# Two paddings in SBUF: 96 bytes at its right end and 64 in the pool of constants

## The chip, the cores and the metric

One core of a Trainium2 chip runs the whole kernel as one launch. The metric is the time of one execution in microseconds of the device. TensorE (PE) multiplies, its weight loads (PEld) run beside the matmuls, VectorE (DVE), ScalarE (ACT) and GpSimd (POOL) do the elementwise work, and nearly all DMAs are issued by the SP queue.

## The reference, cut to what matters

One layer over 2048 latent tokens and 256 context tokens, width 1024, 8 heads of 128:

```python
hx = layernorm(x) * (1 + scale_x) + shift_x          # ctx likewise, with c_ctx
px = hx @ w_in + b_in                                # 10272 columns: q k v, z_a, decay logits, x_in, b_gate, c_gate, z_b, g_a, g_b
q, k, v = silu(conv3(qkv))                           # q and k normalised
o = gated_delta_rule(q, k, v, g, beta)               # both directions, from the context's final state
y_a = rmsnorm(o) * o_norm_w * silu(z_a)
y_b = b_gate * (conv3(c_gate * x_in) + conv_b_b) * silu(z_b)
merged = sigmoid(g_a) * (y_a @ w_a) + sigmoid(g_b) * (y_b @ w_b)
out = layernorm(2 ** 0.25 * x + gate_x * (merged @ w_out)) * ln_g + ln_b
```

## The kernel before

**Three stages.** After a start of about 100 us (shift and scale, normalised tokens, the first right-hand operands) `projections` multiplies by `w_in` until about 1840 us. Then `window` runs the delta-rule scan of 36 visits, with the products by `w_b` and `w_a` put between the scan's matmuls as fillers, until a little after 3000 us. Then `final` multiplies by `w_out` and normalises.

**A dense product** is made in float32r, with each operand split into a high and a low part, and costs three matmuls instead of one: high by high, high by low, low by high. One matmul has a stationary operand of 128 by 128, which a weight load brings into the array, and a moving operand of 128 by 512, which streams through it. Every matmul of a dense product has its own weight load.

**The projections** are made in Winograd's form by `strassen`: 80 units (40 for each pair of token tiles), each a pair of column tiles of `w_in`. A unit has seven products in the order `ORDER = "1675243"`, a product has four tiles of k, and each tile has the three matmuls of L743 to L745:

```python
mm(ps, hi[:, k, :], bh, ...)   # L743: stationary ah, moving bh
mm(ps, hi[:, k, :], bl, ...)   # L744: stationary ah, moving bl
mm(ps, lo[:, k, :], bh, ...)   # L745: stationary al, moving bh
```

That is 12 matmuls a product, 84 a unit and 6720 in all. The moving operands `bh`, `bl` of a product stay in SBUF through a pair's 40 units. Those of the products 1, 6, 7, 5 and 2 lie in pool `bp`, at the right end of SBUF; those of the products 4 and 3 (`LATE`) lie in pool `bq`, at the left. The stationary operands `ah`, `al` of the next unit are made while the current one runs, by ACT (the high part) and POOL (the low part) in `split`, in pool `ap`. The first 12 units of each pair give k, v and q; there PE also transposes what was finished (L1013), and for the values it makes the context's products in plain float32 (L792). The 28 units behind them give branch B and the gates.

**The fillers** (L1227, L1229, L1231; 1536 matmuls) have moving operands in pool `fa` and stationary ones in pool `wp`, both at the right end. The last products (L1574 to L1576; 672 matmuls) have moving operands in pool `bo` and stationary ones in `o0` and `o1`, all at the left. The scan's own matmuls are plain float32; each shows as two matmuls in the trace.

**What sets the addresses.** Pools are stacks: those of the left side grow up from the constants' pool `cp`, those of the right side grow down from the end of SBUF. A tile's *start* here is its byte offset within a partition, and its *phase* is that start modulo 128. As the tiles of the dense products have sizes that are multiples of 512 bytes, all tiles of one pool have the same phase.

Of the kernel before, what the change touches and what calls it, by code (L numbers as in the profile page):

```python
# [15 lines left out]
P = 128  # L16
D = 1024
KT = 8
H = 8
# [13 lines left out]
def bc(ap, n):  # L33
    """[p, a, 1] -> [p, a, n] by a zero stride."""
    return ap.to_broadcast([ap.shape[0], ap.shape[1], n])


class Kern:
# [6 lines left out]
    # ---------------------------------------------------------------- constants  # L45
    def consts(self, pool, tmp):
# [23 lines left out]
        # strict parts of a 16 x 16 block  # L70
# [5 lines left out]
        # inclusive causal masks [j, i]: 0 where kept, NEG elsewhere  # L76
# [9 lines left out]
    # ---------------------------------------------------------------- gated delta net  # L86
# [10 lines left out]
    def visit_load(self, v):  # L97
        """Loads of a chunk's keys, values, queries and running decays."""
# [21 lines left out]
    def visit_decay(self, v):  # L120
        """Decays: of every key to the chunk's end, of the state over the chunk, and between positions."""
# [23 lines left out]
    def gram(self, v, name, rhs):  # L145
        """Products of a chunk's keys, the same for both directions: kept in DRAM for the second."""
# [7 lines left out]
        for g in range(2):  # L154
# [4 lines left out]
            if v["latent"]:  # L159
                # with the other direction's strengths  # L160
# [9 lines left out]
    # R = (I + N)^-1 of each head's triangular N (its strict part; upper for d = 0)  # L170
    def inv_base(self, v):
        nc, g2, d, N = self.nc, self.g2, v["d"], v["N"]
        # the 32 x 32 diagonal blocks, negated
# [9 lines left out]
        # substitution within the 16 x 16 blocks  # L183
# [50 lines left out]
    def blocks(self, d, b):  # L234
        """(rows of the solved block, rows of the other) of every pair of b x b blocks."""
        lo, hi = (0, 1) if d == 0 else (1, 0)
        return [(slice(2 * b * g + b * lo, 2 * b * g + b * lo + b), slice(2 * b * g + b * hi, 2 * b * g + b * hi + b))
                for g in range(P // (2 * b))]
# [51 lines left out]
    # the recurrence  # L290
# [44 lines left out]
    # ---------------------------------------------------------------- dense helpers  # L335
    def load_w(self, src, c0, n=P):
        """W[:, c0:c0+n] as [128 k, 8, n], and its split into two float32r parts."""
# [11 lines left out]
    def split(self, hi, lo, src, eng=None):  # L349
        """hi + lo == src, each with the significant bits that a float32r pass carries."""  # L350
# [3 lines left out]
    def dense(self, ps, w, a, msl=slice(None), nsl=slice(None)):  # L354
        """ps[m, n] = sum_k w[k, m] a[k, n], operands in two float32r parts."""
# [7 lines left out]
    # ---------------------------------------------------------------- whole kernel  # L363
    def build(self, I, out):
# [3 lines left out]
        self.w_in = I["w_in"][0]  # L368
        cp = es.enter_context(tc.tile_pool(name="cp", bufs=1))
        dr = es.enter_context(tc.tile_pool(name="dr", bufs=1, space=DRAM))  # L370
# [37 lines left out]
        def settle():  # L408
            """Room for the scan."""
# [16 lines left out]
    # ---------------------------------------------------------------- the input projections  # L426
    def projections(self, es, eb, cp):
        """All products with w_in: the context's plainly, the latents' by pairs of token tiles (Winograd's form)."""
# [58 lines left out]
    def tokens_of(self, t):  # L487
        """A tile of latent tokens, two blocks at a time; the first where the second's operands will be."""
# [4 lines left out]
    def units(self, pair):  # L493
        """Column pairs of w_in in their order, each with what becomes of its four blocks
        and what comes before it and after it."""
        nc = self.nc
        cols = lambda seg, m: 4128 + seg * 1024 + m * P     # x_in, b_gate, c_gate, z_b, g_a, g_b
# [21 lines left out]
        # q, k, v; the context's values beside the latents'  # L519
# [14 lines left out]
        # branch B  # L534
# [50 lines left out]
        # gates  # L585
# [7 lines left out]
        for seg, dst in ((5, self.gb_d), (4, self.ga_d), (None, self.za_d)):  # L593
            for m in range(0, 8, 2):
                def evac(i, j, src, seg=seg, dst=dst, m=m):
                    b = (24 + m if seg is None else bcol(seg, m)) + i
                    zs = ph["ev"].tile([P, 512], F32, name="c11") if (i, j) == (0, 0) else src
                    if seg is None:
                        nc.scalar.activation(out=zs, in_=src, func=AF.Silu, bias=bT[:, b:b + 1])
                        # the last ones behind the activations, out of the way of the scan's loads  # L600
# [8 lines left out]
        if pair == 0:  # L609
            # the other pair's tokens, on the way  # L610
# [19 lines left out]
    # Winograd's form for C = W^T H with W^T = [[A11, A12], [A21, A22]] by (column tile, half of k) and  # L630
    # H = [[B11, B12], [B21, B22]] by (half of k, token tile):
    #   s1 = A21 + A22, s2 = s1 - A11, s3 = A11 - A21, s4 = A12 - s2
    #   t1 = B12 - B11, t2 = B22 - t1, t3 = B22 - B12, t4 = t2 - B21
    #   p1 = A11 B11, p2 = A12 B21, p3 = s4 B22, p4 = A22 t4, p5 = s1 t1, p6 = s2 t2, p7 = s3 t3
    #   C11 = p1 + p2, C12 = p1 + p6 + p5 + p3, C21 = p1 + p6 + p7 - p4, C22 = p1 + p6 + p7 + p5
    def prep_b(self, k):
        """The first pair's right-hand operands, a tile of k of each half."""
# [16 lines left out]
    def turn_pair(self, xs, q, k):  # L654
        """The second pair's operands of a block of tokens of each tile and a tile of k of each half, kept in DRAM."""
# [11 lines left out]
    def renew(self):  # L667
        """The second pair's operands in the place of the first's, each as soon as its last product is done."""
# [17 lines left out]
    def gate_rows(self, pool):  # L686
        """c's rows times the residual gate's columns of w_mod, by the two float32r parts of c."""
# [135 lines left out]
    def later(self, n, fn):  # L823
        """fn, n products from now."""
        self.due.append((self.tick + n, fn))
# [8 lines left out]
    # ---------------------------------------------------------------- startup  # L834
    def modulation(self, cp, wmp):
        """Small operands, the shifts and scales, and the first tokens."""
# [30 lines left out]
        # shift and scale: rows first, then channels on partitions; some tiles of k in float32r parts  # L867
# [756 lines left out]
```

## Time and profile before

| | us |
|---|---|
| median of 3 runs | 3305.19 |
| fastest and slowest | 3304.52, 3312.04 |
| span of the profiled execution | 3301.7 |
| PE busy in it | 3035.6 (92%) |
| DVE busy | 2283.1 (69%) |
| POOL busy | 1628.0 (49%) |
| ACT busy | 1561.9 (47%) |

The span is the time from the first to the last instruction. The time of the profiled execution as a whole is not listed apart; the shortest of the runs, 3304.52 us, is 2.8 us above the span, the median 3.5 us. Busy time of PE is a modelled one: matmuls overlap in the array, and one of 128x512 is shown as lasting about 0.39 us although the next one starts about 0.23 us after it. So the rate of a row of matmuls is read from their starts, in the timeline, and not from their durations.

### The profile page before, as it was taken

Reading aid. Unit: us, or ns where it says so; the run is one execution under the profiler, and the core shown is the slowest. Engines: PE = TensorE matmul, PEld = TensorE weight load, DVE = VectorE, ACT = ScalarE, POOL = GpSimd, SP = SyncE. Lnnn points to the kernel's source line nnn. Section 1 sums busy time; section 2 is a strip of 40 time slices with the busy share of each in tenths; the row PEclk is TensorE's granted clock in tenths of the full one; section 3 lists DMA queues with packets and bytes.
Section 4 is the critical chain, followed back from the end, with each engine's and each line's share of the span. In section 5 each row is a group of like instructions: output and inputs, shape, how many; then the busy total and the mean of one; then the engine's idle time right before and its main releaser. Section 6 shows DMA issues by size and latency. Waiting matters only on the chain.

```text
span 3301.7 us, 60541 instructions
## 1 busy us (share of the span) xinstructions
PE 3035.6 (92%) x22089; PEld 2484.4 (75%) x22089; DVE 2283.1 (69%) x5815; ACT 1561.9 (47%) x3453; POOL 1628.0 (49%) x1156
## 2 busy tenths in 40 slices
PE   7899999999998999999999888888889888898988
PEld 3677777788886777888878677887777777776766
DVE  7656545555646564555622678899898989978699
ACT  4664633333456555333434355555555665664321
POOL 3444557665576554666666333343343233424464
PEclk9999999999999999999999988889999989999999
DMA  5533322225564432222332654465566667667742
GB/s 210 142 99 96 95 80 87 74 64 156 173 186 136 115 93 76 64 64 65 98 108 86 214 172 150 167 196 170 174 205 212 212 216 239 219 209 241 228 146 102
DMA packets 423047, 481.75 MB, mean 146 GB/s; under 512 B 25428, under 2 KB 324949, under 8 KB 421724
## 3 DMA queue, kind: packets, MB, share of 16 engines
q1 hardware_dynamic: 413646, 470.43, 45.5%
q10 hardware_dynamic: 9102, 7.45, 0.7%
q8 instruction: 173, 2.83, 0.4%
q14 instruction: 126, 1.03, 0.1%
HBM read 341.32 MB, written 136.47 MB: 145 GB/s over the span
## 4 chain that ended last, share of the span: by engine, by line
PE 52%; DVE 25%; issue 6%; ACT 5%; DMA 5%; POOL 3%; SPq 1%; DVEq 0%; ACTq 0%; POOLq 0%
PE pd L743 13%; PE pd L744 13%; PE pd L745 13%; DVE gcb L140 3%; DVE rb L192 3%; DVE R L193 2%; POOL al L352 2%; DVE rb L191 2%; DMA gcb<-gcd 1%; PE pst L319 1%; ACT n L177 1%; POOL s L729 1%; DVE N L167 1%; PE pst L320 1%; DVE t L988 1%
## 5 line engine op out<-in xcount | busy, mean ns | idle before, releaser
L743 PE MATMUL pd<-bh,ah 128*128 128x512 f32 x2240 | 898.0, 401 | 9.8 <-ACT u L763 5.3
L745 PE MATMUL pd<-bh,al 128*128 128x512 f32 x2240 | 886.3, 396 | 0.0
L744 PE MATMUL pd<-bl,ah 128*128 128x512 f32 x2240 | 886.3, 396 | 0.0
L352 POOL TENSOR_TENSOR al<-s,ah 128x512 fp32r<-128x512 f32 x348 | 478.1, 1376 | 427.6 <-ACT ah L351 408.5
L352 POOL TENSOR_TENSOR al<-raw,ah 128x512 fp32r<-128x512 f32 x260 | 372.7, 1436 | 339.4 <-ACT ah L351 296.1
L743 PEld LDWEIGHTS pd<-bh,ah 128*128 128x128 f32 x2240 | 423.5, 189 | 107.2 <-issue 6.4
L745 PEld LDWEIGHTS pd<-bh,al 128*128 128x128 f32 x2240 | 423.5, 189 | 99.7 <-DVE al L352 0.4
L744 PEld LDWEIGHTS pd<-bl,ah 128*128 128x128 f32 x2240 | 424.0, 189 | 94.2
L351 ACT CAST ah<-s 128x512 fp32r<-128x512 f32 x352 | 215.0, 618 | 358.7 <-PE pd L744 342.8
L351 ACT CAST ah<-raw 128x512 fp32r<-128x512 f32 x264 | 162.5, 617 | 263.7 <-PE pd L744 213.8
L729 DVE TENSOR_TENSOR s<-s,raw 128x512 f32<-128x512 f32 x80 | 97.0, 1213 | 218.0 <-POOL s L729 161.5
L1231 PE MATMUL pf<-ah,wl 128*128 128x512 f32 x512 | 221.8, 433 | 6.7 <-DVE wl L352 4.6
L1227 PE MATMUL pf<-ah,wh 128*128 128x512 f32 x512 | 214.2, 419 | 12.4 <-DVE R L193 5.0
L1229 PE MATMUL pf<-al,wh 128*128 128x512 f32 x512 | 214.8, 420 | 5.9 <-POOL al L352 3.0
L352 POOL TENSOR_TENSOR wl<-wraw,wh 128x1024 fp32r<-128x1024 f32 x48 | 115.9, 2416 | 197.5 <-ACT wh L351 66.5
L192 DVE TENSOR_TENSOR rb<-rb,n 128x8 f32<-128x8 f32 (+6 forms) x540 | 200.8, 373 | 5.0
L140 DVE SCALAR_TENSOR_TENSOR gcb<-gcb,gc,mask 128x128 f32<-128x128 f32 x288 | 178.0, 623 | 9.1 <-ACT qd L137 8.1
L138 POOL TENSOR_TENSOR qd<-qd,qT 128x1024 f32<-128x1024 f32 x32 | 76.4, 2386 | 202.8 <-ACT qd L137 199.2
L193 DVE TENSOR_TENSOR R<-R,rb 128x8 f32<-128x8 f32 (+6 forms) x540 | 158.1, 294 | 5.6
L319 PE MATMUL pst<-S,qd 128*128 128x128 f32 x512 | 112.2, 304 | 33.7 <-ACT ot L1265 17.0
L768 DVE TENSOR_TENSOR u<-pd,u 128x512 f32<-128x512 f32 x80 | 55.0, 687 | 116.7 <-PE pd L745 113.6
L1005 ACT ACTIVATE t<-t 128x512 f32<-128x512 f32 (+1 forms) x112 | 67.3, 601 | 141.2 <-DVE t L990 141.2
(346 smaller groups left out, 6242.2 us busy)
## 6 DMA issues: line engine op xcount, KB each, us to landing
raw<-in_w_in SPq DMA_DIRECT2D x160, 512.0 KB, 4.0
kT<-kTd SPq DMA_DIRECT2D x36, 512.0 KB, 5.1
gcb<-gcd SPq DMA_DIRECT2D x36, 512.0 KB, 4.1
kt<-kd SPq DMA_DIRECT2D x36, 512.0 KB, 4.5
vh<-vd SPq DMA_DIRECT2D x36, 512.0 KB, 4.3
wraw<-in_w_b SPq DMA_DIRECT2D x32, 512.0 KB, 5.0
qT<-qTd SPq DMA_DIRECT2D x32, 512.0 KB, 3.9
wraw<-in_w_a SPq DMA_DIRECT2D x32, 512.0 KB, 5.2
```

The source lines that it names most:

```text
L140: nc.vector.scalar_tensor_tensor(out=gcb[:, h, :], in0=gcb[:, h, :], scalar=gcT[:, h:h + 1], in1=self.mask[d], op0=ALU.subtract, op1=ALU.min)
L192: nc.vector.tensor_tensor(out=rbv, in0=rbv, in1=bc(n16[:, :, i:i + 1], w), op=ALU.mult)
L193: nc.vector.tensor_tensor(out=R[:, :, c0:c1], in0=R[:, :, c0:c1], in1=rbv, op=ALU.add)
L319: nc.tensor.matmul(po[:, j, :], v["qd"][:, h, :], S[:, h, :], start=True, stop=False)
L351: self.nc.scalar.copy(out=hi, in_=src)
L352: (eng or self.nc.gpsimd).tensor_tensor(out=lo, in0=src, in1=hi.bitcast(F32), op=ALU.subtract)
L743: mm(ps, hi[:, k, :], bh, start=(first and k == 0), stop=False, skip_group_check=not first)
L744: mm(ps, hi[:, k, :], bl, start=False, stop=False, skip_group_check=not first)
L745: mm(ps, lo[:, k, :], bh, start=False, stop=(last and k == 3), skip_group_check=not first)
L1227: mm(ps, wh[:, k, :], ah, start=(k == 0), stop=False)
L1229: mm(ps, wh[:, k, :], al, start=False, stop=False)
L1231: mm(ps, wl[:, k, :], ah, start=False, stop=(k == KT - 1))
```

## The change

Two tiles are allocated that nothing writes or reads. One of 24 floats (96 bytes) is in a pool of its own at the right end of SBUF, opened ahead of all other pools. The other, of 16 floats (64 bytes), is the first in the pool of constants. Nothing else is changed but comments and docstrings, which are left out here:

```diff
     def build(self, I, out):
         tc, nc, es = self.tc, self.nc, self.es
         self.I = I
         x2 = I["x"][0]
         self.w_in = I["w_in"][0]
+
+        es.enter_context(tc.tile_pool(name="edge", bufs=1, side="right")).tile([P, 24], F32, name="edge")
         cp = es.enter_context(tc.tile_pool(name="cp", bufs=1))
+        cp.tile([P, 16], F32, name="cpad")
         dr = es.enter_context(tc.tile_pool(name="dr", bufs=1, space=DRAM))
```

On every engine the instructions, their order and their semaphores are the same in both programs, instruction by instruction. What differs is addresses: every tile of the left side starts 64 bytes higher, every tile of the right side 96 bytes lower. The phases, as the two built programs place the tiles:

| matmuls | moving, before → after | stationary, before → after |
|---|---|---|
| L743 to L745, products 1 6 7 5 2 (4800) | `bp` 96 → 0 | `ap` 64 → 0 |
| L743 to L745, products 4 3 (1920) | `bq` 64 → 0 | `ap` 64 → 0 |
| fillers (1536) | `fa` 96 → 0 | `wp` 96 → 0 |
| last products (672) | `bo` 64 → 0 | `o0`, `o1` 64 → 0 |
| L886, L887 at the start (24) | `wm` 0 → 32 | `cr4` in `cp` 16, 48, 112 → 80, 112, 48 |
| L792, the context's values, float32 | `hc` 96 → 0 | `ap` 64 → 0 |
| L1043, the context's keys, float32 | `hc` 96 → 0 | `wp` 96 → 0 |
| scan, float32: L299 / L319 | `S` 32 → 96 | `kT` 96 → 0 / `qd` 64 → 0 |

The constants in `cp` (the identity, the masks, the biases) move by 64, the scan's pool `g1` from 32 to 96, `g2` and `gb` from 64 to 0.

## Rows read from the trace of the kernel before

**Rows 1.** The page: its head, and groups of section 5 (columns as named there)

```profile
span 3301.7 us, 60541 instructions
...
L743 PE MATMUL pd<-bh,ah 128*128 128x512 f32 x2240 | 898.0, 401 | 9.8 <-ACT u L763 5.3
...
L744 PE MATMUL pd<-bl,ah 128*128 128x512 f32 x2240 | 886.3, 396 | 0.0
```

**Rows 2.** Busy time by stretch: us, PE, PEld, DVE, ACT, POOL, clock, DMA, GB/s

```profile
425.00:985.00 560.00, 559.53 (x2453) 450.22 (x2453) 302.92 (x438) 217.84 (x379) 367.60 (x269) 1.00 0.39 116
985.00:1312.00 327.00, 302.64 (x1364) 236.88 (x1363) 188.82 (x311) 186.10 (x497) 178.24 (x131) 0.97 0.38 107
1312.00:1841.00 529.00, 527.93 (x2275) 427.17 (x2275) 240.29 (x297) 188.21 (x303) 320.02 (x240) 1.00 0.28 84
```

**Rows 3.** Chain that ended last, by line, from 420 to 1850 us

```profile
by line: PE pd L743 27.7%; PE pd L744 27.7%; PE pd L745 27.6%; issue 3.7%; POOL al L352 2.0%; DVE t L988 1.4%; PE pd L1077 1.2%; POOL s L729 1.2%; DVE t L990 1.1%; PE pt L1013 1.0%; DVE t L1003 0.6%; DVE s L729 0.5%; PE pt L659 0.5%; ACT t 
```

**Rows 4.** Timeline of PE in one unit: start us, us, instruction

```profile
1448.19 0.40 PE L743 MATMUL pd<-bh,ah 128*128 128x512 f32 x1
...
1462.24 0.39 PE L743 MATMUL pd<-bh,ah 128*128 128x512 f32 x1
...
1463.62 0.39 PE L743 MATMUL pd<-bh,ah 128*128 128x512 f32 x1
...
1467.70 0.40 PE L743 MATMUL pd<-bh,ah 128*128 128x512 f32 x1
```

**Rows 5.** Busy time by stretch, columns as in rows 2: two products, then fillers

```profile
1459.43:1462.24 2.81, 2.81 (x13) 2.26 (x12) 0.75 (x1) 0.62 (x1) 2.59 (x3) 1.00 0.00 0
...
1465.00:1467.70 2.70, 2.70 (x13) 2.24 (x12) 0.75 (x1) 0.64 (x2) 1.29 (x1) 1.00 0.01 3
1860.77:1869.38 8.61, 8.61 (x39) 7.13 (x38) 8.37 (x28) 2.23 (x3) 4.78 (x2) 1.00 0.82 284
```

**Rows 6.** Timeline of PE: fillers in a row, from their second

```profile
1858.92 0.40 PE L1229 MATMUL pf<-al,wh 128*128 128x512 f32 x1
...
1860.77 0.39 PE L1227 MATMUL pf<-ah,wh 128*128 128x512 f32 x1
...
1869.38 0.39 PE L1231 MATMUL pf<-ah,wl 128*128 128x512 f32 x1
```

**Rows 7.** Timeline of PE: last products

```profile
3115.30 0.39 PE L1574 MATMUL po<-oh,ah 128*128 128x512 f32 x1
...
3117.57 0.39 PE L1575 MATMUL po<-ol,ah 128*128 128x512 f32 x1
```

**Rows 8.** Timeline of PE: plain float32, rows of equal matmuls merged

```profile
74.32 5.78 PE L1043 MATMUL pd<-hc,wraw 128*128 128x256 f32 x26
...
207.48 3.62 PE L792 MATMUL pd<-hc,raw 128*128 128x256 f32 x16
```

**Rows 9.** Waits of PE, 985 to 1312 us: waiter, waited for, us, times, longest

```profile
PE pt L1013 <- ACT t L1005: 17.0, 11, 3.9
```

**Rows 10.** Chain that ended last, by line, from 140 to 330 us

```profile
by line: issue 20.1%; PE pd L792 10.9%; POOL al L352 9.6%; PE pd L745 8.8%; PE pd L743 8.8%; PE pd L744 8.8%; POOL s L729 6.0%; DVE t L988 4.5%; DVE s L729 4.4%; DVE t L990 2.8%; PE pt L1013 2.7%; DVE t L1003 2.5%; DMA raw<-in_w_in 2.1%; AC
```

**Rows 11.** Groups of POOL by line, columns as in rows 1

```profile
L352 POOL TENSOR_TENSOR al<-s,ah 128x512 fp32r<-128x512 f32 x348 | 478.1, 1376 | 427.6 <-ACT ah L351 408.5 <-PE po L1575 12.2 <-DMA kd<-tk 2.0
...
L352 POOL TENSOR_TENSOR al<-yr,ah 128x512 fp32r<-128x512 f32 x51 | 67.9, 1344 | 65.3 <-ACT ah L351 56.5 <-DMA yr<-yad 7.1 <-PE pd L745 1.7
```

**Rows 12.** Timeline of PE at the start, narrow weights

```profile
16.58 0.39 PE L886 MATMUL pd<-wmh,cr 128*4 128x512 f32 x1
...
18.20 0.40 PE L887 MATMUL pd<-wml,cr 128*2 128x512 f32 x1
```

**Rows 13.** The scan by stretch: stretch, us, PE busy (instructions), clock, DMA, GB/s

```profile
1841.00:3000.00 1159.00, 1006.47 (x13232) 0.91 0.61 199
```

**Rows 14.** Busy time by stretch, columns as in rows 2: one product behind a wait

```profile
1118.28:1121.50 3.22, 3.22 (x11) 2.55 (x10) 2.91 (x6) 2.61 (x5) 1.87 (x2) 0.51 0.01 3
```

## Prediction, made before the changed kernel ran

> **What bounds the kernel now.** I read the page first: of a span of 3301.7 us the groups of L743 to L745, 2240 matmuls each, are the dearest work [rows 1]. Then the busy time by stretch, to see where PE is the limit. In the two stretches that hold branch B and the gates, 56 of the 80 units, PE is busy 559.5 of 560 us and 527.9 of 529 us, at full clock, with POOL, the next, at 368 and 320 us; in the second pair's k, v and q it is busy 302.6 of 327 us [rows 2]. The chain that ended last, from 420 to 1850 us, is made to 83% of these three lines (27.7 + 27.7 + 27.6) [rows 3]. So in 56 units the distance from one matmul's start to the next sets the time, and that is what the change can touch.
>
> That distance is not one number. In a unit of the gates the 60 matmuls of products 1, 6, 7, 5, 2 start from 1448.19 to 1462.24 us: 14.05 / 60 = 0.2342 us each. Of the 24 behind them, products 4 and 3, the first six take 1.38 us (0.230 each) and the other 18 run from 1463.62 to 1467.70 us: 4.08 / 18 = 0.2267 us [rows 4]. Same engine, shapes, lines and stationary pool; only the moving operands' pool differs.
>
> Is it what runs beside it? The busy time by stretch answers: product 2 takes 2.81 us for 12 with a DMA share of 0.00, product 3 takes 2.70 with 0.01, and the fillers keep their pace with a share of 0.82 and 284 GB/s [rows 5]. Those fillers need 1.85 us for their first 8 steps (0.231) and then 8.61 for 38 (0.2266), with both operands at phase 96 [rows 6]. The last products take 2.27 us for 10 (0.227), both at 64 [rows 7]. So phase 96 is not slow in itself, nor is the right end of SBUF. What sets the five slow products apart is that the moving operand stands at 96 and the stationary one at 64: phases that differ. With equal phases the row settles, after about nine matmuls, at 0.2267; with 96 against 64 it stays at 0.2342. I read this as the two streams of reads getting in each other's way; the rows show the rhythm, not the cause.
>
> Plain float32 does not care: 26 matmuls with 96 against 96 take 5.78 us, 16 with 96 against 64 take 3.62; less the last one's 0.38 that is 0.216 a step in both [rows 8].
>
> **The change part by part.** It adds no instruction, moves none and adds no wait; padding costs nothing by itself. Its two paddings give all dense products 0 against 0.
>
> *Products 1, 6, 7, 5, 2 in the 56 units.* 60 x (0.2342 - 0.2267) = 0.45 us a unit, and 0.02 of the run-in of product 4, which no longer has to settle: 0.47. 56 x 0.47 = 26.3 us. Where PE does something else between two products the run-in starts again and costs 9 x 0.004 = 0.04 us; I put 40 such breaks in these units (transposes of the other tokens, gate rows), 1.5 us. That leaves 24.8. All of it is on the path, as PE never waits there. What would be late next is POOL, at 66% of the stretch, so a unit 2.4% shorter leaves it room.
>
> *The 24 units of k, v, q.* The same 0.45 a unit, less four or five breaks for transposes (0.18): 0.27, in all 6.5 us at most. But here PE also waits: 17.0 us for ACT's t in the second pair's stretch, in 11 waits [rows 9], and the chain from 140 to 330 us has 20.1% of issue, 9.6% of POOL's split and 6.0% of its sums [rows 10]. Where another engine's loop sets the pace, PE that is faster only waits longer. Bounds 0 and 6.5; I take 3.5, the middle, as about half of these units run without such a wait.
>
> *Fillers, last products, products 4 and 3.* Equal phases before and after: 0. The float32 work: 0 [rows 8], also for `S` against `kT`, whose difference goes from 64 to 96.
>
> *Other engines.* POOL's split lasts 1376 ns on tiles at 64 and 1344 ns on those at 96 [rows 11], a difference smaller than what contention does to the means; all starts stay multiples of 32. I take 0.
>
> *Narrow weights at the start.* 24 matmuls at 0 against 16, 48 and 112 take 1.62 us for 7 (0.231) [rows 12]; whatever they become, it is under 0.2 us.
>
> Sum: 24.8 + 3.5 = 28 us off the span, 3301.7 to 3274. Around the span lie 2.8 to 10.3 us by the runs shown, 3.5 for the median; with that the time is 3305.2 - 28 = 3277 us. Bounds of the mechanism: 24.8 - 4 (breaks and waits twice as dear) = 21 at the least, 26.3 + 6.5 + 3 (run-ins) = 36 at the most: 3269 to 3284. On top comes the scan, whose chain is made of many waits at a mean clock of 0.91 [rows 13]: begun 28 us earlier it meets the clock's falls elsewhere, which I put at 6 us either way on the slow side and 3 on the fast.
>
> **The rivals.**
>
> *No change: addresses are not the cause.* Then products 1 to 2 differ from 4 and 3 by their place in the unit, and the time stays 3305. For it: the two always come in this order. Against: product 2, without any DMA, has the slow pace and product 4 begins to settle six matmuls later [rows 4, 5], and fillers and last products settle wherever they stand. The Trainium skill speaks for this rival: "TensorE: Matmul & The Clock Gate", section "Back-to-back issue gap", gives the distance between matmuls as a function of the columns alone, about 216 ns for 512, and part 2 of that page says that a weight load takes no read bandwidth from the running matmul; "SBUF — State Buffer", in its specifications, has lines of 16 bytes, of which all these phases are multiples. By these rules the padding would be worth 0 and the time 3305. The trace disagrees with the first: the same line has two distances here, 234 and 227, and neither is 216.
>
> *Slower: phase 0 does not settle.* No row before shows 0 against 0 with full weights; the one at 0 runs at 0.231 and does not settle [rows 12]. If what counts is not the difference but the place within 128 bytes, and 0 is a bad place, the five products keep 0.234 and all that runs at 0.227 now loses: 80 units x 24 x 0.0075 = 14 us, 672 last products 5 us, a part of the fillers 4 us: 3305 + 23 = 3328. It decides if rows at 0 against 0 stay above 0.231. Against: 64 and 96 settle at the same 0.2267, and the narrow weights at 0 stand against 16, 48 and 112, which is a difference again.
>
> *Given back behind.* PE that finishes a product sooner waits longer for k, v and q, and a long wait is followed by half the clock: behind a wait for ACT at 1118 us the granted clock was 0.51, the lower of its two levels (1.2 GHz), for 3.2 us [rows 14], 1.6 us lost. Twelve to fifteen more such falls, there or in the scan, would eat 20 us or more: 3297 to 3305. Now the mean clock from 985 to 1312 us, 0.97 [rows 2], leaves room for some 20 us at the lower level in all, four or five such falls; three times as many is unlikely.
>
> *More than I count.* If 0 against 0 settles lower than 0.2267, each 0.001 us is worth 6.7 us in the projections alone; with 0.224, 18 us more: 3259. Nothing in the rows points there, as 64 and 96 settle at one value.
>
> **How the numbers follow.** Forecast as worked out (21 to 36 us off): 0.84. More: 0.03. No change because addresses don't matter: 0.05. Given back: 0.03. Phase 0 does not settle: 0.05. A measurement of this kernel can tell about 0.3% from no change, 10 us. The first two are faster by more than that, 0.87; the next two within it, 0.08; the last is slower, 0.05. The range is that of the forecast with the scan's play: 3269 - 3 to 3284 + 6, so 3266 to 3290; that leaves out the other cases and the ends of this one, under 0.2 in all.
>
> **What would show each step.** Right: in the gates' units the starts of products 1, 6, 7, 5, 2 stand 0.2267 apart, a unit takes 19.04 us (84 x 0.2267) instead of 19.51, L743 and L744 have means nearer 390 ns, and the scan begins 26 to 32 us earlier. Wrong: a unit still of 19.5 us (no change), products 4 and 3 above 0.230 (0 does not settle), or a stage of 1841 us that is shorter while the rest of the span is longer by as much (given back). If k, v and q gain nothing, or all of 6.5 us, my middle was wrong and the mechanism stands. If the scan's matmuls change their distance, float32 was not as indifferent as I took it.

## The result, and the profile after

The changed kernel takes **3277.9 us** (median; 3274.0 to 3286.1), the kernel before beside it 3308.0 (3304.2 to 3313.9): a ratio of 0.9913, with a 95% interval from 0.9896 to 0.993. The profiled execution took 3284.18 us, at the slow end of these, with a span of 3282.5; the one of before has a span of 3301.7, and with the 1.7 us that lie around it here it comes to 3303.4, less than the shortest of its runs. From profile to profile only 19.2 of the 30 us are seen, and the two have to be told apart below.

The page of the changed kernel, its head and the three dear groups (L743, L744, L745 of before are L746, L747, L748 here), beside [rows 1]:

```profile
span 3282.5 us, 60541 instructions
...
L746 PE MATMUL pd<-bh,ah 128*128 128x512 f32 x2240 | 889.1, 397 | 9.9 <-ACT u L766 5.8
L748 PE MATMUL pd<-bh,al 128*128 128x512 f32 x2240 | 877.7, 392 | 0.0
L747 PE MATMUL pd<-bl,ah 128*128 128x512 f32 x2240 | 876.8, 391 | 0.0
```

The modelled means fall by 4 to 5 ns, from 401 and 396 for L743 and L744 to 397 and 391 for the same lines here, L746 and L747. The rate stands in the timeline. Here is PE in the unit that [rows 4] show of before, the first of its 84 matmuls, the first of product 4 and the first of the next unit (start us, us, instruction):

```profile
1438.08 0.39 PE L746 MATMUL pd<-bh,ah 128*128 128x512 f32 x1
...
1451.68 0.39 PE L746 MATMUL pd<-bh,ah 128*128 128x512 f32 x1
...
1457.12 0.39 PE L746 MATMUL pd<-bh,ah 128*128 128x512 f32 x1
```

Products 1, 6, 7, 5, 2 need 13.60 us for 60 starts, 0.2267 each (before: 14.05, 0.2342). Products 4 and 3 need 5.44 for 24, also 0.2267, without the run-in that they had. The unit takes 19.04 us instead of 19.51.

**The whole account.** Both spans are cut where the same instruction starts: the first dense product, the first product of branch B in the first pair, the first k unit of the second pair, its first unit of branch B, the first filler, the end. So the counts of instructions agree row by row. First before, then after, columns as in [rows 2]:

```profile
0.00:100.53 100.53, 74.73 (x316) 41.54 (x317) 76.07 (x192) 46.05 (x94) 33.34 (x33) 0.97 0.60 206
100.53:423.42 322.89, 304.81 (x1403) 239.90 (x1403) 197.52 (x356) 184.85 (x495) 154.43 (x114) 0.99 0.36 104
...
423.42:987.05 563.63, 563.16 (x2469) 453.21 (x2468) 302.96 (x438) 219.65 (x382) 369.65 (x270) 1.00 0.39 116
...
987.05:1289.38 302.33, 278.45 (x1249) 217.19 (x1248) 184.42 (x302) 173.69 (x459) 165.44 (x122) 0.97 0.40 112
...
1289.38:1840.70 551.32, 549.78 (x2380) 444.87 (x2378) 244.34 (x304) 198.66 (x336) 330.48 (x247) 1.00 0.27 81
1840.70:3301.70 1461.00, 1264.63 (x14276) 1087.66 (x14276) 1277.74 (x4225) 739.00 (x1689) 574.66 (x372) 0.92 0.60 194
```

```profile
0.00:103.30 103.30, 78.87 (x316) 45.36 (x316) 76.39 (x193) 47.12 (x95) 32.35 (x33) 0.92 0.60 205
103.30:429.10 325.80, 305.13 (x1403) 241.76 (x1403) 196.45 (x355) 184.13 (x494) 154.26 (x114) 0.98 0.36 102
...
429.10:980.95 551.85, 551.37 (x2469) 452.14 (x2468) 307.82 (x438) 218.19 (x382) 368.83 (x270) 1.00 0.40 119
...
980.95:1282.84 301.89, 276.26 (x1249) 216.82 (x1248) 183.54 (x302) 174.06 (x459) 165.34 (x122) 0.97 0.40 112
...
1282.84:1821.20 538.36, 536.82 (x2380) 443.96 (x2378) 251.50 (x304) 198.54 (x336) 326.13 (x247) 1.00 0.28 83
...
1821.20:3282.50 1461.30, 1263.43 (x14276) 1086.55 (x14276) 1279.02 (x4225) 738.21 (x1689) 575.82 (x372) 0.92 0.59 194
```

| stretch | before | after | difference |
|---|---|---|---|
| start | 100.53 | 103.30 | +2.8 |
| k, v, q of the first pair | 322.89 | 325.80 | +2.9 |
| branch B and gates, first pair | 563.63 | 551.85 | -11.8 |
| k, v, q of the second pair | 302.33 | 301.89 | -0.4 |
| branch B and gates, second pair | 551.32 | 538.36 | -13.0 |
| scan and final stage | 1461.00 | 1461.30 | +0.3 |

The two stretches in which PE never waits give 24.7 us. The rest gives nothing back and gains nothing, but for 5.7 us at the start and in the first k, v and q, where the granted clock was lower this time (0.92 for 0.97, then 0.98 for 0.99). By the trace's record of the clock its lower level (1.2 GHz) lasted 17.1 us in this start, 6.8 before, and then 10.2 us against 3.4. The lower level is half of the upper one, so the 10.3 and 6.8 us that came on top can cost up to 5.1 and 3.4 us (an estimate); 2.8 and 2.9 were lost.

### The profile page after: what moved, and what is told of

Read it like the earlier page. It is cut to its first block, busy times and chain, and to the rows that moved or that the text cites. A ratio compares the mean times of both kernels' runs of the same rounds, so it can differ in the third digit from the quotient of the medians.

```text
span 3282.5 us, 60541 instructions
## 1 busy us (share of the span) xinstructions
PE 3011.9 (92%) x22089; PEld 2486.6 (76%) x22089; DVE 2294.7 (70%) x5815; ACT 1560.3 (48%) x3453; POOL 1622.7 (49%) x1156
## 4 chain that ended last, share of the span: by engine, by line
PE 50%; DVE 26%; issue 6%; ACT 5%; DMA 4%; POOL 4%; SPq 0%; DVEq 0%; ACTq 0%; POOLq 0%
PE pd L746 12%; PE pd L747 12%; PE pd L748 12%; DVE rb L192 3%; DVE gcb L140 3%; DVE R L193 2%; POOL al L352 2%; DVE rb L191 2%; DMA gcb<-gcd 2%; PE pf L1234 1%; PE pf L1230 1%; PE pf L1232 1%; DVE N L167 1%; PE pst L319 1%; ACT n L177 1%
## 5 line engine op out<-in xcount | busy, mean ns | idle before, releaser
L746 PE MATMUL pd<-bh,ah 128*128 128x512 f32 x2240 | 889.1, 397 | 9.9 <-ACT u L766 5.8
L748 PE MATMUL pd<-bh,al 128*128 128x512 f32 x2240 | 877.7, 392 | 0.0
L747 PE MATMUL pd<-bl,ah 128*128 128x512 f32 x2240 | 876.8, 391 | 0.0
L746 PEld LDWEIGHTS pd<-bh,ah 128*128 128x128 f32 x2240 | 423.6, 189 | 98.1 <-issue 6.6
L748 PEld LDWEIGHTS pd<-bh,al 128*128 128x128 f32 x2240 | 423.2, 189 | 90.3 <-POOL al L352 0.4
L747 PEld LDWEIGHTS pd<-bl,ah 128*128 128x128 f32 x2240 | 423.6, 189 | 85.5
L732 DVE TENSOR_TENSOR s<-s,raw 128x512 f32<-128x512 f32 x80 | 111.8, 1397 | 217.8 <-POOL s L732 217.8
L319 PE MATMUL pst<-S,qd 128*128 128x128 f32 x512 | 113.4, 307 | 36.5 <-ACT ot L1268 18.2
```

Source lines behind the costliest of these rows:

```text
L319: nc.tensor.matmul(po[:, j, :], v["qd"][:, h, :], S[:, h, :], start=True, stop=False)
L746: mm(ps, hi[:, k, :], bh, start=(first and k == 0), stop=False, skip_group_check=not first)
L747: mm(ps, hi[:, k, :], bl, start=False, stop=False, skip_group_check=not first)
L748: mm(ps, lo[:, k, :], bh, start=False, stop=(last and k == 3), skip_group_check=not first)
```

## The experiments

The theory of the prediction was: the five slow products are slow because their moving and stationary operands start at different phases modulo 128. The first rival: what counts is that both begin on multiples of 128, as they do after the change. In the kernels of the layer below only addresses differ from before, but for the one with the stationary operands moved: there three early loads of weights on the SP queue also wait for other instructions than before. "Moving" and "stationary" are the starts for products 1, 6, 7, 5, 2.

### Single pairs of starts

The rows of equal matmuls were made in one small kernel, which slices two tiles:

```
row(mv[:, m // 4:m // 4 + 512], st[:, s // 4:s // 4 + 128], 40)   # for each pair (m, s) in bytes
```

In the built program both tiles begin 128 bytes above a multiple of 512. The starts given below are counted from there; a difference of two starts is not touched by it, nor is what is a multiple of 128.

> Not the layer: only rows of 40 equal float32r matmuls (128 columns of weights, 512 moving columns, each with its own weight load), one row for each pair of starts (moving, stationary), with one small float32 matmul between rows, then a few rows of plain float32 and of bfloat16; the output is a constant. Starts are slices of two tiles, so that the difference takes all multiples of 32 bytes from 0 to 480, and 4, 8, 16, 48, 112; some pairs stand at (32,0), (64,0), (96,0), (96,64), (64,96), (32,32), (16,16), (4,4), (64,32), (480,64). Theory (the difference of the two starts modulo 128 decides): rows with a difference of 0, 128, 256 and 384 settle at 0.2267 us from start to start after about nine matmuls, so do (32,32), (16,16), (4,4); differences of 32 and 96, and all that leave 32 or 96 modulo 128, stay at 0.234; 64 is open, by the rows of before it may be either. Rival, multiples of 128 decide: (32,32), (16,16), (4,4) stay at 0.234 and only pairs whose both starts are multiples of 128 settle. Rival, a difference modulo 64: 64, 192, 320 settle too, and 32 and 96 read alike. Rival, addresses do not matter: all rows settle at 0.2267. Plain float32, 256 columns: 0.216 for each matmul shown in every row, by the theory and by all rivals.

Timeline of PE in this kernel, the ends of ten of its rows, one line each: start of the first matmul shown, us to the end of the last, count. In order: stationary minus moving 0, 32, 64, 96, 128, 192, 256 (moving at 0), then both at 32, both at 16, both at 4; last two rows of plain float32, with differences of 0 and 32.

```profile
28.17 5.38 PE L46 MATMUL t<-mv,st 128*128 128x512 f32 x23
...
37.81 5.30 PE L46 MATMUL t<-mv,st 128*128 128x512 f32 x22
...
47.14 5.53 PE L46 MATMUL t<-mv,st 128*128 128x512 f32 x23
...
56.94 5.31 PE L46 MATMUL t<-mv,st 128*128 128x512 f32 x22
...
66.50 5.28 PE L46 MATMUL t<-mv,st 128*128 128x512 f32 x22
...
85.53 5.20 PE L46 MATMUL t<-mv,st 128*128 128x512 f32 x22
...
104.48 5.15 PE L46 MATMUL t<-mv,st 128*128 128x512 f32 x22
...
275.75 5.16 PE L46 MATMUL t<-mv,st 128*128 128x512 f32 x22
...
285.10 5.22 PE L46 MATMUL t<-mv,st 128*128 128x512 f32 x22
...
294.43 5.63 PE L46 MATMUL t<-mv,st 128*128 128x512 f32 x23
...
319.26 6.21 PE L46 MATMUL t<-one 128*128 128x256 f32 x28
...
325.52 6.21 PE L46 MATMUL t<-one 128*128 128x256 f32 x28
```

A row's end holds the last matmul's own 0.39 us, so the first reads (5.38 - 0.39) / 22 = 0.2268, the fourth (5.31 - 0.39) / 21 = 0.2343. The mean of the last 21 distances of each row, from the starts in the trace:

| stationary - moving, bytes | us from start to start |
|---|---|
| 0, 256 | 0.2267 |
| 192, 448 | 0.2289 |
| 128, 384 | 0.2323, 0.2324 |
| 32, 64, 160, 224, 288, 320, 416, 480 | 0.2332 to 0.2334 |
| 96, 352 | 0.2343 |
| both at 32; at 16; at 4 | 0.2267; 0.2300; 0.2378 |

My theory falls here, and so does the rival. A difference of 128 does not settle, though both starts are then multiples of 128; 256 does. Both at 32 settle too. The table repeats with a period of **256**, not 128. Moving it as a whole changes nothing: 32 against 0 gives 0.2334 like 0 against 480. Plain float32, with 256 columns, stays at 0.216 for each matmul shown. So does bfloat16 with 512 columns and a weight load for each matmul; two of its rows, with differences of 0 and 96:

```profile
344.32 8.80 PE L46 MATMUL t<-bm,bs 128*128 128x512 bf16 x39
...
370.89 8.80 PE L46 MATMUL t<-bm,bs 128*128 128x512 bf16 x39
```

A row has 40 matmuls, of which one stands in no record of the trace: (8.80 - 0.39) / 39 = 0.216 in both.

### Only the stationary operands moved, by 32

```diff
         self.ap = self.pool(es, "ap")
+        self.ap.tile([P, 8], F32, name="apad")
```

> The kernel before with one pad of 32 bytes ahead of the stationary operands' pool (and so of what lies above it on the left), and nothing else: products 1, 6, 7, 5, 2 then have 96 against 96, products 4 and 3 have 64 against 96. Theory (equal phases settle): the slow and the fast products change places: 60 starts at 0.2267 and 24 at 0.234 in a unit, so 13.60 + 5.62 = 19.22 us instead of 19.51, 0.29 us off each of 56 units, 16 us, and -2 to +3 in k, v and q: 3288 to 3294 beside a kernel before of 3308, ratio 0.994 to 0.996. Rival, multiples of 128 decide: nothing here begins on one, units stay at 19.51, ratio 1.000. Rival, the place in the unit decides: products 1, 6, 7, 5, 2 stay at 0.234, 4 and 3 at 0.2267, ratio 1.000. Rival, 96 on the right end is a bad place for a moving operand whatever stands against it: as the last one, ratio 1.000, and products 4 and 3 unchanged.

Measured: ratio 0.9998 (0.9984 to 1.0013). In the timeline the unit, from its first start to the next one's:

```profile
1449.88 0.39 PE L744 MATMUL pd<-bh,ah 128*128 128x512 f32 x1
...
1469.43 0.39 PE L744 MATMUL pd<-bh,ah 128*128 128x512 f32 x1
```

19.55 us. The five products are at 0.2316 to 0.2330, not at the 0.2267 that I expected; products 4 and 3 are at 0.2332 to 0.2335, so the place in the unit is not what makes them fast. By modulo 128 the five are equal; by 256 they differ by 128. The expectation failed, and the table above has both numbers.

### All at 64, by 32 bytes at the right end

```diff
+        es.enter_context(tc.tile_pool(name="edge", bufs=1, side="right")).tile([P, 8], F32, name="edge")
         cp = es.enter_context(tc.tile_pool(name="cp", bufs=1))
```

> The kernel before with a pad of 32 bytes at the right end alone: all dense products then have 64 against 64, and no pool of matmul operands begins on a multiple of 128. Theory (equal phases settle, wherever they are): units of 19.04 us as with both paddings, 56 x 0.47 = 26 us less 1.5 for breaks, ratio 0.990 to 0.993, the same time as the changed kernel within 0.2%. Rival, multiples of 128 decide: units of 19.51 us, ratio 1.000. Rival, the constants' shift by 64 bytes is what helped (the scan, the transposes): ratio above 0.995 with a stage of projections that is no shorter.

Measured: ratio 0.9975 (0.9962 to 0.9989), and

```profile
1446.82 0.40 PE L744 MATMUL pd<-bh,ah 128*128 128x512 f32 x1
...
1466.26 0.40 PE L744 MATMUL pd<-bh,ah 128*128 128x512 f32 x1
```

19.45 us a unit: a miss. All dense products have 64 against 64 modulo 128, and nearly all the gain is missing. By itself this run would have spoken for the rival, multiples of 128. But the moving operands stand at 192 and the stationary ones at 64 modulo 256, 128 apart, as in the run before it. Four of the five products take 0.2333 here, the table's row for 128 is 0.2323; the layer's matmuls change between two moving and two stationary tiles, and what the 0.001 comes from isn't shown.

### Two kernels that set 256 against 128

The first has only 160 bytes at the right end: no pool of dense operands begins on a multiple of 128, the difference is 0 modulo 256. The second is the changed kernel with 128 bytes more at the right end (56 floats for 24): all pools of dense operands begin on multiples of 128, the difference is 128 modulo 256.

```diff
-        es.enter_context(tc.tile_pool(name="edge", bufs=1, side="right")).tile([P, 24], F32, name="edge")
+        es.enter_context(tc.tile_pool(name="edge", bufs=1, side="right")).tile([P, 40], F32, name="edge")
         cp = es.enter_context(tc.tile_pool(name="cp", bufs=1))
-        cp.tile([P, 16], F32, name="cpad")
```

> The kernel before with a pad of 160 bytes at the right end alone. The moving operands of products 1, 6, 7, 5, 2 then start at 64 modulo 128 and at 320 modulo 512, the stationary ones at 64: no pool of operands begins on a multiple of 128, but the difference is a multiple of 256. New theory (the rows with single pairs of starts: only a difference of 0 modulo 256 settles at 0.2267, 128 stays at 0.232, 32 and 96 at 0.233 to 0.234): units of 19.04 to 19.06 us, the 56 units together 24 to 26 us shorter than before, ratio 0.990 to 0.993. My theory of the prediction, a difference modulo 128: the same. Rival, multiples of 128 decide: units of 19.45 to 19.51 us, ratio 0.997 to 1.000.

> The changed kernel with 128 bytes more at the right end (224 instead of 96) and the same 64 bytes in the pool of constants: every pool of matmul operands still begins on a multiple of 128, but the moving operands of products 1, 6, 7, 5, 2 stand 128 bytes from the stationary ones modulo 256. New theory (modulo 256): these five products are back at 0.232 to 0.234, products 4 and 3 at 0.2267, units of 19.40 to 19.50 us, ratio to before 0.996 to 1.000: the gain is gone. My theory of the prediction (modulo 128) and the rival that multiples of 128 decide: units of 19.04 us, ratio 0.990 to 0.993, as with 96 bytes.

Measured: 0.9919 (0.9894 to 0.9944) for the first, 0.9993 (0.9974 to 1.0011) for the second. The unit in the first, then in the second:

```profile
1434.04 0.39 PE L744 MATMUL pd<-bh,ah 128*128 128x512 f32 x1
...
1453.08 0.39 PE L744 MATMUL pd<-bh,ah 128*128 128x512 f32 x1
```

```profile
1453.18 0.40 PE L745 MATMUL pd<-bh,ah 128*128 128x512 f32 x1
...
1472.63 0.40 PE L745 MATMUL pd<-bh,ah 128*128 128x512 f32 x1
```

19.04 against 19.45 us. The whole gain, 24.8 us in the 56 units, is there without a single one of these pools on a multiple of 128, and all but 3.6 us of it is gone with all of them there. That decides it against both modulo 128 and the rival.

### The changed kernel again

> The changed kernel once more, on the chip of the two runs beside it, for a second profile of the same program. Units of branch B and the gates of 19.04 us again, the 56 together 551 to 552 us up to the k units of the second pair and 538 behind them, ratio 0.990 to 0.993. Open is the stage of k, v and q, where the first profile of the changed kernel lost 2.9 us in the first pair and gained 0.4 in the second: if these belong to falls of the clock they come out otherwise here (-3 to +3), and units at full clock are as long as before within 0.1 us; if the new addresses cost something there, the loss of 3 us in the first pair comes again.

Ratio 0.9925 (0.9904 to 0.9946). Its units take 19.04 us again, and its 56 units, 551.87 and 538.33 us by the same cuts, repeat the 551.85 and 538.36 of the first profile to 0.03 us. The first pair's k, v and q took 324.2 us, against 325.8 in the first profile and 322.9 before; the lower level of the clock lasted 6.8, 10.2 and 3.4 us in them. The loss did come out otherwise, and with the clock, but not at nothing.

### Finer starts, fewer columns, no gap

> Again not the layer, but rows of 40 equal float32r matmuls for each pair of starts, with a constant as output: moving at 0 against stationary at 0, 16, 32 ... 256, 24, 184, 200, 248, 252; both at one start from 0 to 256 in steps of 32, at 8 and at 48; differences of 256 from starts 0, 64, 128, 192; some pairs of a difference of 128 or -64; then rows of 256 and of 128 moving columns, and three rows without anything between them, at differences 96, 0, 96. New theory: of the multiples of 16 only 0 and 256 settle at 0.2267, whatever the common start is as long as it is a multiple of 32; 192 (that is -64) stays near 0.229, 128 at 0.232, all others at 0.233 to 0.235. In the three rows without a gap the pace changes with the pair, 0.234, then 0.2267 after up to twelve matmuls, then 0.234, with nothing left over from the row ahead. Rival, some place has a pace under 0.226 (0.216, that of plain float32): then a better pair of starts exists than that of the changed kernel. Rival, the history of the row ahead sets the pace: the second of the three rows stays at 0.234.

Moving at 0, the stationary start at 16 or 48 gives 0.2332 and 0.2333, at 240 0.2284, at 248 and 252 0.2333. Of the multiples of 16, 80 (0.2321), 176 (0.2300) and 240 miss the 0.233 to 0.235 that I expected. Equal starts at 0, 32, 64 and on to 256 all settle at 0.2267, at 8 and 48 they stay at 0.2311. No pair is below 0.2267, so no better place for these operands was found. The ends of three rows that follow each other without a gap, with differences of 96, 0 and 96, and then two rows of 256 columns, with differences of 0 and 32:

```profile
449.81 5.31 PE L42 MATMUL t<-mv,st 128*128 128x512 f32 x22
...
459.08 5.15 PE L42 MATMUL t<-mv,st 128*128 128x512 f32 x22
...
468.51 5.08 PE L42 MATMUL t<-mv,st 128*128 128x512 f32 x21
```

```profile
421.20 5.04 PE L42 MATMUL t<-mv,st 128*128 128x256 f32 x40
...
426.22 4.98 PE L42 MATMUL t<-mv,st 128*128 128x256 f32 x40
```

0.2343, 0.2267, 0.2345: the pace follows the pair (the second row has settled nine matmuls in), and nothing is left over from the row ahead. With 256 columns the equal pair is no faster: 0.120 against 0.118 from start to start, over the last 21 distances. So the rule is shown for 512 columns alone.

### Each padding alone

```diff
+        es.enter_context(tc.tile_pool(name="edge", bufs=1, side="right")).tile([P, 24], F32, name="edge")
         cp = es.enter_context(tc.tile_pool(name="cp", bufs=1))
```

> The right end's 96 bytes alone, without the 64 in the pool of constants: the moving operands of products 1, 6, 7, 5, 2 start at 384 modulo 512, the stationary ones at 64, so the stationary start lies 192 (-64) behind modulo 256. Theory (modulo 256, with the rows of single pairs of starts as a table): 0.229 us for these five products, units of 60 x 0.229 + 24 x 0.2267 = 19.18 us, up to 19.30 where high and low parts alternate less well; 56 units 12 to 19 us shorter than before, ratio 0.9935 to 0.997: some two thirds of the gain. Theory of the prediction (modulo 128, 64 against 0): no statement; rival, multiples of 128 of the moving operand decide: the whole gain, 0.990 to 0.993; rival, both must be multiples of 128: none, 1.000. Start of the projections: 102.5 to 103.5 us if the right end's shift by 96 or more brings the later start seen in four kernels, 100.5 to 101.3 if that was chance or needs the other shift.

```diff
         cp = es.enter_context(tc.tile_pool(name="cp", bufs=1))
+        cp.tile([P, 16], F32, name="cpad")
```

> The 64 bytes in the pool of constants alone: moving operands of the five products at 480 modulo 512, stationary ones at 128, a difference of 160 modulo 256. Theory (modulo 256, table): 0.2333 for these products, units of 19.42 to 19.50 us, ratio 0.996 to 1.000: next to nothing. Rival, multiples of 128 of the stationary operand decide: the whole gain. Rival, the two paddings add up, each worth its part: the ratio here and that of the right end's padding alone, multiplied, give 0.991 to 0.993. Start of the projections: 100.5 to 101.3 us, as the right end is not moved.

Measured: the right end alone 0.9966 (0.995 to 0.9981), the constants alone 0.9989 (0.9971 to 1.0007). The unit with the right end's padding alone:

```profile
1442.03 0.40 PE L744 MATMUL pd<-bh,ah 128*128 128x512 f32 x1
...
1461.27 0.40 PE L744 MATMUL pd<-bh,ah 128*128 128x512 f32 x1
```

19.24 us, with four of the five products at 0.2288 and product 1 at 0.2304: the table's 0.2289 for a difference of 192. With the constants' padding alone the unit takes 19.49 us. The two do not add up: 0.9966 times 0.9989 is 0.9955, and 56 units give 15.0 and 1.1 us, not 24.8. They bring two differences to zero together. The later start, 103.3 and 103.6 us, came in both, and with the constants' padding I had expected 100.5 to 101.3; so it isn't the right end's.

### One pad of 160 bytes, at either end

```diff
         cp = es.enter_context(tc.tile_pool(name="cp", bufs=1))
+        cp.tile([P, 40], F32, name="cpad")
```

> A single pad of 160 bytes in the pool of constants, nothing at the right end: stationary operands at 224 modulo 512, moving ones of the five products at 480, a difference of 256; nothing begins on a multiple of 128 (all these pools are at 96). Theory (modulo 256): units of 19.04 us, the 56 units 24.8 us shorter than before, ratio 0.990 to 0.993. Rival, multiples of 128: ratio 1.000. Start of the projections: 100.5 to 101.3 us if the later start belongs to the shift of the right end, and then the profile's span is 3275 to 3280; 102.5 to 103.5 if it comes with this pace of the projections or by chance.

> The pad of 160 bytes at the right end once more, on one chip with the pad of 160 bytes in the pool of constants beside it. Both have a difference of 256 and units of 19.04 us, so the 56 units should again be 24.7 to 24.8 us shorter than before, ratio 0.990 to 0.994. By the theory the two kernels differ by nothing in the projections' 56 units; if this one is again faster by 8 to 10 us, the difference must lie in the start, in k, v and q, or in the scan, and the rows of these stretches should show it; if it is chance, the two ratios come within 0.003 of each other.

> The pad of 160 bytes in the pool of constants once more: the first time it gave a ratio of 0.9944, above the 0.990 to 0.993 that was expected, with all of the 24.8 us in its 56 units. Chance: 0.990 to 0.994 now. A real cost of these addresses elsewhere (constants, scan): 0.994 to 0.996 again, with the stretch behind the projections or k, v and q longer by 5 to 8 us than in the kernel beside it.

With the pad in the constants, all at 96 modulo 128, the unit takes 19.04 us again:

```profile
1437.00 0.39 PE L744 MATMUL pd<-bh,ah 128*128 128x512 f32 x1
...
1456.04 0.39 PE L744 MATMUL pd<-bh,ah 128*128 128x512 f32 x1
```

The ratios were 0.9944 (0.9924 to 0.9965) and, again, 0.993 (0.9914 to 0.9947); for the right end again 0.9914 (0.9899 to 0.993). The first is above what I expected. The intervals overlap, the two kernels' second ratios are 0.0016 apart, and their 56 units are equal to 0.03 us, so chance is not excluded; but the first pair's k, v and q took 326.5 and 327.4 us in the two profiles with the pad in the constants, and 322.8 and 322.9 in those with the pad at the right end. In the first two the clock was at its lower level for 10.2 us of this stretch, in the other two for 6.8. Half of the 3.4 us between them would be 1.7 of the 4 us (an estimate); whether the rest is lost by these addresses stays open (below).

### All of them together

| kernel | moving, stationary mod 256 | difference | unit, us | 56 units shorter by, us | ratio (interval) |
|---|---|---|---|---|---|
| before | 224, 64 | 96 | 19.51 | | |
| both paddings | 128, 128 | 0 | 19.04 | 24.7 | 0.9913 (0.9896 to 0.993) |
| both, again | 128, 128 | 0 | 19.04 | 24.8 | 0.9925 (0.9904 to 0.9946) |
| right end 160 | 64, 64 | 0 | 19.04 | 24.8 | 0.9919 (0.9894 to 0.9944) |
| constants 160 | 224, 224 | 0 | 19.04 | 24.8 | 0.9944 (0.9924 to 0.9965) |
| right end 96 | 128, 64 | 192 | 19.24 | 15.0 | 0.9966 (0.995 to 0.9981) |
| right end 32 | 192, 64 | 128 | 19.45 | 3.6 | 0.9975 (0.9962 to 0.9989) |
| right end 224, constants 64 | 0, 128 | 128 | 19.45 | 3.6 | 0.9993 (0.9974 to 1.0011) |
| constants 64 | 224, 128 | 160 | 19.49 | 1.1 | 0.9989 (0.9971 to 1.0007) |
| stationary 32 | 224, 96 | 128 | 19.55 | -1.9 | 0.9998 (0.9984 to 1.0013) |

The 24.8 us of some 3307 are 0.0075. The mean of the six ratios at a difference of 0, with the second ones of the two kernels with 160 bytes (0.9914 and 0.993), is 0.9924, which is what the 56 units give.

## Why the prediction was right, and where it was not

**What bounds the kernel: right.** Where PE never waits, 24.7 us were gained in the 56 units; where it waits, nothing was.

**The rule behind the sum: wrong, with the right value here.** "With equal phases the row settles" took phases modulo 128. The rows of before could not tell: every pair that settled there was equal modulo 256 as well, and the only unequal one with full weights, 96 by either count, was slow. The change happens to make the difference 256; the same paddings with 128 bytes more gave 3.6 of the 24.8 us, and I would have forecast the same 3277 us for them. The run with 32 bytes at the right end is that mistake, made: 0.9975 where I wrote 0.990 to 0.993.

**Products 1, 6, 7, 5, 2: right in size.** 0.47 us a unit, as worked out, and the run-in of product 4 is gone: 84 x 0.2267 = 19.04. Breaks cost 26.3 - 24.7 = 1.6 us, where I had put 1.5.

**k, v and q: wrong.** I took 3.5 us, the middle between 0 and 6.5; in these two profiles the stretches come out 2.9 us longer and 0.4 shorter, and where the clock stayed up the gain is 0.02 a unit. Two of these units whose clock stayed up, first before, then after:

```profile
343.34 0.48 PE L743 MATMUL pd<-bh,ah 128*128 128x512 f32 x1
...
365.16 0.48 PE L743 MATMUL pd<-bh,ah 128*128 128x512 f32 x1
```

```profile
348.85 0.48 PE L746 MATMUL pd<-bh,ah 128*128 128x512 f32 x1
...
370.65 0.47 PE L746 MATMUL pd<-bh,ah 128*128 128x512 f32 x1
```

21.82 against 21.80 us, though the products in it are faster (the first four take 0.2380 from start to start on the mean, 0.2414 before). The same two units by busy time, columns as in [rows 2]:

```profile
343.34:365.16 21.82, 21.67 (x104) 17.22 (x102) 13.06 (x24) 14.89 (x49) 12.40 (x9) 1.00 0.36 97
```

```profile
348.85:370.65 21.80, 21.41 (x104) 17.18 (x102) 13.06 (x24) 14.87 (x49) 12.38 (x9) 1.00 0.37 97
```

PE is idle for 0.39 us instead of 0.15, and 0.3 of it is a wait for ACT's `t`. In these units another loop sets the pace, and PE waits longer for what it gained: the bound at 0 was the right one, and the chain's issue, split and sums [rows 10] spoke for it. "About half of these units" had no row behind it.

**Fillers, last products, float32, other engines: right at 0.** Scan and final stage took 1461.0 and 1461.3 us with the same 14276 matmuls.

**The sum.** 28 us were forecast, the profiles give 19.2, the medians 30.1, the ratio 0.9913 is 28.8 of 3308. The mechanism gives 24.7 of it. That the total came so near is luck as well: the interval of the ratio holds 23 to 34 us, and what lies outside the 56 units changes by more than 3.5 us from execution to execution. The kernel with 160 bytes at the right end has 1459.9 us behind the projections in one profile and 1469.6 in the other, the same program both times. My 6 and 3 us for the scan's play were of that kind, and rather too small. What I put around the span, 2.8 to 10.3 us, was this too: the times were those of other executions, and each run's own time is 1.7 us above its span.

**The rivals.** *Addresses are not the cause* fell: in kernels that differ by addresses, and in the rows of the small kernel, the pace follows one number of bytes. The Trainium skill, "TensorE: Matmul & The Clock Gate", section "Back-to-back issue gap", gives the gap of an isolated matmul from its columns alone, 216 ns for 512, and about 131 ns for each of a stream of weight loads and matmuls of 512 columns. The rows of this case agree with the first for bfloat16, 0.216 us in a stream with weight loads, and disagree for float32r, 0.2267 to 0.2378 for the same 512 columns; no row shows the second. Plain float32, 0.216 for 256 columns, was no test of it. *Phase 0 does not settle* fell, as the changed kernel's 0 against 0 gives 0.2267. *Given back behind* did not decide, though 5.7 us were lost ahead of 429 us in this profile, beside more falls of the clock. *More than I count* fell: no float32r row of 512 columns is under 0.2267.

## What to carry to other kernels

Look at the distance from start to start, not at the shown duration, and compare rows of the same instruction: two paces at full clock with nothing beside them point at the operands' addresses. Then measure the pairs of starts by themselves before choosing a pad; one small kernel gave the period of 256 that the large one could not show, and a single pad of 160 bytes at the right end does the same as the two of this change. And a faster PE pays only in stretches in which PE never waits: take such a term at its lower bound where another engine's loop sets the pace.

## What was not expected of the hardware

- For float32r with 512 moving columns and a weight load for each matmul, the pace depends on stationary minus moving start modulo 256: 0.2267 at 0, 0.2289 at 192, 0.2323 at 128, 0.2332 to 0.2343 at the other multiples of 32; in the layer 128 gave 0.2316 to 0.2333. With equal starts the common start counts only where it isn't a multiple of 32: 0.2267 at all multiples of 32, 0.2300 at 16, 0.2311 at 8 and 48, 0.2378 at 4. What in the reads of the two operands makes this pattern isn't shown by any run here.
- It does not show for float32r with 256 or 128 columns (0.120 against 0.118, and 0.112 in both), nor for bfloat16 with 512 columns or plain float32 with 256 (0.216 in all rows).
- The start of the projections comes at 100.5 to 101.3 us in the four profiles with 6.8 us at the lower level of the clock ahead of it, at 101.7 to 103.6 in the eight with 17.1. The kernel with 160 bytes in the constants had both, with the same program. Its two profiles, from 40 to 60 us:

```profile
40.00:60.00 20.00, 12.20 (x60) 9.17 (x60) 19.62 (x74) 13.99 (x23) 5.20 (x5) 0.83 0.10 28
```

```profile
40.00:60.00 20.00, 13.36 (x60) 10.23 (x60) 18.97 (x69) 13.91 (x23) 4.83 (x4) 0.74 0.11 28
```

  In a wait of PE of 5.0 us the granted clock fell to the lower level (1.2 GHz), for 6.8 us in the first and 10.2 in the second: a mean of 0.83 and 0.74 over these 20 us. Two more falls of 3.4 us followed in the second ahead of the projections, none in the first. Why the clock took two courses isn't shown.
- In the twelve profiles the first pair's k, v and q took 324.2 to 327.4 us in the six with a pad in the constants and 322.4 to 324.0 in the six without. The first unit there takes 30.8 to 32.1 us in the five with 10.2 us at the lower level in this stretch and 29.1 to 29.7 in the seven with 3.4 or 6.8; both kinds of kernel had both. At 6.8 us the stretch is 324.2 and 325.0 us long with the pad and 322.8 to 323.2 without, at 10.2 it is 325.8 to 327.4 with it and 324.0 in the one without. So the clock accounts for a part only, and whether the constants' addresses cost the 1 to 3 us that are left isn't settled.
